# Gradient clipping by global norm: smaller last pieces, two engines for the squares, and a shorter scalar chain between load and store

## Chip, cores, metric

One NeuronCore of a Trainium2 chip. The metric is the device time of one execution in microseconds (us). Executions of one kernel agree within some 0.3 to 0.6%. A profile's span (50.5 us for the kernel before) is about 1.8 us shorter than the time of the same run. In the profile's lines PE is TensorE (PEld its weight load), DVE is VectorE, ACT ScalarE, POOL GpSimd and SP SyncE, whose queue issues the transfers; a q behind an engine's name is its sequencer, and L47 is line 47 of that run's kernel. A transfer has landed when its semaphore (the counter that those who need the data wait for) says so. The dots in the profile's fences mark lines left out.

## The reference

```python
grad: (512, 4096) float32      # 8.39 MB
norm  = np.sqrt(np.sum(grad ** 2))
scale = min(1.0, max_norm / (norm + 1e-8))     # max_norm = 1.0
return (grad * scale).astype(np.float32)
```

Every output needs the sum over every input. The whole tensor fits in SBUF, so it is read once and written once.

## The kernel before

```python
F = 2048                                     # nch = 8 chunks of [128, 2048], 1 MB each
gin = flat_in.rearrange("(n p f) -> n p f", p=P, f=F)
...
nc.vector.memset(ones, 1.0)
...
for i in range(nch):                         # 8 loads of 1 MB
    ch = data_pool.tile([P, F], fp32, name=f"ch{i}", tag="ch")
    chunks.append(ch)
    nc.sync.dma_start(out=ch, in_=gin[i])

for i in range(nch):                         # sums of squares, all on VectorE (line 47)
    nc.vector.tensor_tensor_reduce(out=sq, in0=chunks[i], in1=chunks[i], scale=1.0, scalar=0.0,
        op0=mult, op1=add, accum_out=acc[:, i : i + 1])

nc.vector.tensor_reduce(out=s, in_=acc, axis=X, op=add)           # over the 8 columns
nc.tensor.matmul(tot_psum, ones, s, start=True, stop=True)        # over the 128 partitions
nc.scalar.activation(out=nrm, in_=tot_psum, func=Sqrt)
nc.vector.tensor_scalar(out=nrm_eps, in0=nrm, scalar1=1.0e-8, scalar2=None, op0=add)
nc.vector.reciprocal(out=inv, in_=nrm_eps)
nc.vector.tensor_scalar(out=scl, in0=inv, scalar1=float(max_norm), scalar2=1.0, op0=mult, op1=min)

for i in range(nch):                         # scale (line 86) and store
    nc.vector.tensor_scalar(out=chunks[i], in0=chunks[i], scalar1=scl, scalar2=None, op0=mult)
    nc.sync.dma_start(out=gout[i], in_=chunks[i])
```

## Time and profile before

Median 52.33 us of 6 runs (52.23 to 52.41). The lines of the profile are in the prediction below; the table has only the lengths of the five stretches, from the first and last data packets of each block in the trace's DMA records.

| stretch of the kernel before | us |
|---|---|
| start of span to first byte of the load | 1.73 |
| load: first byte to last byte | 20.73 |
| hole: last byte of the load to issue of the first store | 5.86 |
| issue of the first store to its first byte | 0.85 |
| store: first byte to last byte | 20.18 |
| end: last byte to end of the span | 1.17 |

Read it as a sum: the stretches lie one behind another, and all but the load and the store are time in which no byte of the tensor moves. The prediction counts the hole from the moment at which the landing is seen (5.40 us); the table counts from the last byte, 0.46 us earlier.

### The profile page before, as it was taken

Reading aid. Unit: us, or ns where it says so; the run is one execution under the profiler, and the core shown is the slowest. Engines: PE = TensorE matmul, PEld = TensorE weight load, DVE = VectorE, ACT = ScalarE, POOL = GpSimd, SP = SyncE. Lnnn points to the kernel's source line nnn. Section 1 sums busy time; section 2 is a strip of 40 time slices with the busy share of each in tenths; the row PEclk is TensorE's granted clock in tenths of the full one; section 3 lists DMA queues with packets and bytes.
Section 4 is the critical chain, followed back from the end, with each engine's and each line's share of the span. In section 5 each row is a group of like instructions: output and inputs, shape, how many; then the busy total and the mean of one; then the engine's idle time right before and its main releaser. Section 6 shows DMA issues by size and latency. Waiting matters only on the chain.

```text
span 50.5 us, 112 instructions
## 1 busy us (share of the span) xinstructions
PE 0.6 (1%) x2; PEld 0.5 (1%) x2; DVE 28.9 (57%) x29; ACT 1.5 (3%) x2; POOL 0.2 (0%) x4
## 2 busy tenths in 40 slices
PE   0000000000000000000040000000000000000000
PEld 0000000000000000000030000000000000000000
DVE  1000597989898989898929999999900000000000
ACT  4500000000000000000010000000000000000000
POOL 1000000000000000000000000000000000000000
DMA  0679999999999999950000099999999999999980
GB/s 0 104 337 435 448 422 422 422 422 422 435 415 435 441 422 422 428 214 0 0 0 0 0 415 415 415 415 415 415 415 415 415 415 428 428 422 415 435 363 0
DMA packets 2304, 16.78 MB, mean 332 GB/s; under 512 B 256, under 2 KB 256, under 8 KB 256
## 3 DMA queue, kind: packets, MB, share of 16 engines
q1 hardware_dynamic: 2304, 16.78, 80.6%
HBM read 8.39 MB, written 8.39 MB: 332 GB/s over the span
## 4 chain that ended last, share of the span: by engine, by line
DMA 37%; DVE 23%; SPq 6%; DVEq 2%; issue 1%; PE 1%; ACT 0%
DMA ch<-in_grad_dram 37%; DVE ch L86 17%; SPq L44 6%; DVE sq L47 5%; DVEq L124 2%; PE tot L63 1%; ACT nrm L66 0%; DVE inv L74 0%; DVE s L59 0%; DVE nrm_eps L70 0%; DVE scl L76 0%; DVEq L47 0%; DVE acc L47 0%
## 5 line engine op out<-in xcount | busy, mean ns | idle before, releaser
L47 DVE CUSTOM_DVE_ANT_0 sq<-ch 128x2048 f32<-128x2048 f32 x8 | 18.3, 2293 | 6.0 <-DMA ch<-in_grad_dram 6.0
L86 DVE TENSOR_SCALAR ch<-ch,scl 128x2048 f32<-128x2048 f32 x8 | 9.7, 1281 | 0.0
L66 ACT ACT_TABLE_LOAD x1 | 1.3, 1283 | 0.7 <-PEq L110 0.7
L63 PE MATMUL tot<-s,ones 128*128 128x1 f32 x2 | 0.6, 361 | 25.6 <-DVE s L59 25.6
L66 ACT ACTIVATE nrm<-tot 128x1 f32<-128x1 f32 x1 | 0.2, 171 | 24.2 <-PE tot L63 24.2
L63 PEld LDWEIGHTS tot<-s,ones 128*128 128x128 f32 x2 | 0.5, 309 | 25.6 <-DVE s L59 25.6
L47 DVE DVE_READ_ACCUMULATOR2_ANT acc<- 128x1 f32 x8 | 0.7, 83 | 0.0
L70 DVE TENSOR_SCALAR nrm_eps<-nrm 128x1 f32<-128x1 f32 x1 | 0.2, 154 | 0.9 <-ACT nrm L66 0.9
L36 DVE MEMSET ones<- 128x128 f32 x1 | 0.2, 165 | 0.8 <-PEq L110 0.8
L74 DVE RECIPROCAL inv<-nrm_eps 128x1 f32<-128x1 f32 x1 | 0.2, 163 | 0.0
L59 DVE TENSOR_REDUCE s<-acc 128x1 f32<-128x8 f32 x1 | 0.2, 161 | 0.0
L76 DVE TENSOR_SCALAR scl<-inv 128x1 f32<-128x1 f32 x1 | 0.2, 153 | 0.0
L110 POOL MEMSET const-bfloat16-1.0<- 128x1 bf16 x1 | 0.1, 101 | 0.0
L110 POOL MEMSET const-uint8-127<- 128x1 uint8 x1 | 0.1, 101 | 0.0
L110 POOL MEMSET const-float32-0.0<- 128x1 f32 x1 | 0.1, 98 | 0.2 <-issue 0.2
L110 POOL MEMSET const-float32-1.0<- 128x1 f32 x1 | 0.1, 98 | 0.0
## 6 DMA issues: line engine op xcount, KB each, us to landing
ch<-in_grad_dram SPq DMA_DIRECT2D x8, 1024.0 KB, 11.8
out_dram<-ch SPq DMA_DIRECT2D x8, 1024.0 KB, 8.5
```

The source lines that it names most:

```text
L36: nc.vector.memset(ones, 1.0)
L44: nc.sync.dma_start(out=ch, in_=gin[i])
L47: nc.vector.tensor_tensor_reduce(out=sq, in0=chunks[i], in1=chunks[i], scale=1.0, scalar=0.0, op0=mybir.AluOpType.mult, op1=mybir.AluOpTyp ...
L59: nc.vector.tensor_reduce(out=s, in_=acc, axis=mybir.AxisListType.X, op=mybir.AluOpType.add)
L63: nc.tensor.matmul(tot_psum, ones, s, start=True, stop=True)
L66: nc.scalar.activation(out=nrm, in_=tot_psum, func=mybir.ActivationFunctionType.Sqrt)
L70: nc.vector.tensor_scalar(out=nrm_eps, in0=nrm, scalar1=1.0e-8, scalar2=None, op0=mybir.AluOpType.add)
L74: nc.vector.reciprocal(out=inv, in_=nrm_eps)
L76: nc.vector.tensor_scalar(out=scl, in0=inv, scalar1=float(max_norm), scalar2=1.0, op0=mybir.AluOpType.mult, op1=mybir.AluOpType.min,)
L86: nc.vector.tensor_scalar(out=chunks[i], in0=chunks[i], scalar1=scl, scalar2=None, op0=mybir.AluOpType.mult,)
L110: nc = _bacc.Bacc("TRN2", target_bir_lowering=False, num_devices=1)
L124: with _tile.TileContext(nc) as tc:
```

## The change

Its intent is to shorten the hole. The last chunk is cut in two regions of 1024 columns, and the squares of every chunk or region are shared between VectorE and ScalarE, so that little work is left when the last byte has landed. The scalar chain has two VectorE links instead of three. The first region stored is the last that was loaded, in two halves of 512 columns, so that the first store can be issued early. Memsets go to GpSimd, and a dummy square root loads ScalarE's table.

```diff
-    gin = flat_in.rearrange("(n p f) -> n p f", p=P, f=F)
+    widths = [F] * (nch - 1) + [1024, 1024]       # contiguous regions of HBM
...
-    nc.vector.memset(ones, 1.0)
+    nc.gpsimd.memset(ones, 1.0)
+    nc.gpsimd.memset(acc, 0.0)                    # acc has 12 columns
+    sq_v, sq_a = ... bf16                         # scratch output of the squares
+    nc.scalar.activation(out=dummy, in_=dummy, func=Sqrt)
...
-    for i in range(nch): tensor_tensor_reduce(chunks[i])           # VectorE
+    for i in range(6):                            # sq_accum: VectorE, sq_accum_act: ScalarE
+        (sq_accum_act if i % 2 else sq_accum)(chunks[i])
+    sq_accum(chunks[6][:, 0:1024]);  sq_accum_act(chunks[6][:, 1024:2048])
+    sq_accum(chunks[7][:, 0:512]);   sq_accum_act(chunks[7][:, 512:1024])
+    sq_accum(chunks[8][:, 0:576]);   sq_accum_act(chunks[8][:, 576:1024])
...
-    nrm = sqrt(tot); nrm_eps = nrm + 1e-8; inv = 1 / nrm_eps; scl = min(inv * max_norm, 1)
+    nrm = sqrt(tot / (mn * mn)); r = max(nrm, 1); scl = 1 / r
...
+    for c0, c1 in ((0, 512), (512, 1024)):
+        scale_store(chunks[8][:, c0:c1], view(flat_out, 8)[:, c0:c1])
+    for i in (7, 0, 1, 2, 3, 4, 5, 6):
+        scale_store(chunks[i], view(flat_out, i))
```

(Shortened to one line per step; each step is one instruction as in the code above.)

More of the change, by code (lines that the diff above doesn't have):

```diff
@@ L19 @@
     fp32 = mybir.dt.float32
+    bf16 = mybir.dt.bfloat16
     P = nc.NUM_PARTITIONS
+    mn = float(max_norm)
     flat_in = grad.flatten()
@@ L27, with view @@
     nch = total // (P * F)
-    gin = flat_in.rearrange("(n p f) -> n p f", p=P, f=F)
-    gout = flat_out.rearrange("(n p f) -> n p f", p=P, f=F)
-    data_pool = ctx.enter_context(tc.tile_pool(name="data", bufs=nch))
+    widths = [F] * (nch - 1) + [1024, 1024]
+    regions, at = [], 0
+    for w in widths:
+        regions.append((at, w))
+        at += P * w
+    assert at == total
+    def view(flat, r):
+        o, w = regions[r]
+        return flat[o : o + P * w].rearrange("(p f) -> p f", f=w)
@@ L32 @@
+    data_pool = ctx.enter_context(tc.tile_pool(name="data", bufs=1))
     small_pool = ctx.enter_context(tc.tile_pool(name="small", bufs=1))
     psum_pool = ctx.enter_context(tc.tile_pool(name="psum", bufs=1, space=bass.MemoryType.PSUM))
-    ones = small_pool.tile([P, P], fp32, name="ones")
-    nc.vector.memset(ones, 1.0)
-    acc = small_pool.tile([P, nch], fp32, name="acc")
-    sq = small_pool.tile([P, F], fp32, name="sq")
-    chunks = []
-    for i in range(nch):
-        ch = data_pool.tile([P, F], fp32, name=f"ch{i}", tag="ch")
-        chunks.append(ch)
-        nc.sync.dma_start(out=ch, in_=gin[i])
@@ L46 @@
-    for i in range(nch):
+    add = mybir.AluOpType.add
+    mult = mybir.AluOpType.mult
+    maxop = mybir.AluOpType.max
+    Sqrt = mybir.ActivationFunctionType.Sqrt
+    Square = mybir.ActivationFunctionType.Square
+    NR = len(widths)
+    chunks = [
+        data_pool.tile([P, w], fp32, name=f"ch{i}", tag=f"ch{i}")
+        for i, w in enumerate(widths)
+    ]
+    for i in range(NR):
+        nc.sync.dma_start(out=chunks[i], in_=view(flat_in, i))
+    ones = small_pool.tile([P, P], fp32, name="ones")
@@ L47, with sq_accum @@
+    nc.gpsimd.memset(ones, 1.0)
+    NACC = 12
+    acc = small_pool.tile([P, NACC], fp32, name="acc")
+    nc.gpsimd.memset(acc, 0.0)
+    sq_v = small_pool.tile([P, F], bf16, name="sq_v")
+    sq_a = small_pool.tile([P, F], bf16, name="sq_a")
+    dummy = small_pool.tile([P, 1], fp32, name="dummy")
+    nc.gpsimd.memset(dummy, 1.0)
+    nc.scalar.activation(out=dummy, in_=dummy, func=Sqrt)
+    ai = 0
+    def sq_accum(src):
+        nonlocal ai
+        n = src.shape[1]
         nc.vector.tensor_tensor_reduce(
-            out=sq,
@@ L49 @@
-            in0=chunks[i],
-            in1=chunks[i],
+            out=sq_v[:, 0:n],
+            in0=src,
+            in1=src,
             scale=1.0,
             scalar=0.0,
-            op0=mybir.AluOpType.mult,
-            op1=mybir.AluOpType.add,
-            accum_out=acc[:, i : i + 1],
-        )
-    s = small_pool.tile([P, 1], fp32, name="s")
-    nc.vector.tensor_reduce(
-        out=s, in_=acc, axis=mybir.AxisListType.X, op=mybir.AluOpType.add
-    )
+            op0=mult,
+            op1=add,
@@ new lines, in sq_accum, with sq_accum_act @@
+            accum_out=acc[:, ai : ai + 1],
+        )
+        ai += 1
+    def sq_accum_act(src):
+        nonlocal ai
+        n = src.shape[1]
+        nc.scalar.activation(
+            out=sq_a[:, 0:n],
+            in_=src,
+            func=Square,
+            accum_out=acc[:, ai : ai + 1],
+        )
+        ai += 1
+    for i in range(6):
+        (sq_accum_act if i % 2 else sq_accum)(chunks[i])
+    sq_accum(chunks[6][:, 0:1024])
+    sq_accum_act(chunks[6][:, 1024:2048])
+    sq_accum(chunks[7][:, 0:512])
@@ L62 @@
+    sq_accum_act(chunks[7][:, 512:1024])
+    sq_accum(chunks[8][:, 0:576])
+    sq_accum_act(chunks[8][:, 576:1024])
+    assert ai == NACC
+    s_col = small_pool.tile([P, 1], fp32, name="s_col")
+    nc.vector.tensor_reduce(out=s_col, in_=acc, op=add, axis=mybir.AxisListType.X)
     tot_psum = psum_pool.tile([P, 1], fp32, name="tot")
-    nc.tensor.matmul(tot_psum, ones, s, start=True, stop=True)
+    nc.tensor.matmul(tot_psum, ones, s_col, start=True, stop=True)
     nrm = small_pool.tile([P, 1], fp32, name="nrm")
-    nc.scalar.activation(
-        out=nrm, in_=tot_psum, func=mybir.ActivationFunctionType.Sqrt
-    )
@@ L69 @@
-    nrm_eps = small_pool.tile([P, 1], fp32, name="nrm_eps")
-    nc.vector.tensor_scalar(
-        out=nrm_eps, in0=nrm, scalar1=1.0e-8, scalar2=None, op0=mybir.AluOpType.add
-    )
-    inv = small_pool.tile([P, 1], fp32, name="inv")
-    nc.vector.reciprocal(out=inv, in_=nrm_eps)
-    scl = small_pool.tile([P, 1], fp32, name="scl")
-    nc.vector.tensor_scalar(
-        out=scl,
-        in0=inv,
-        scalar1=float(max_norm),
-        scalar2=1.0,
-        op0=mybir.AluOpType.mult,
-        op1=mybir.AluOpType.min,
-    )
@@ L85 @@
-    for i in range(nch):
-        nc.vector.tensor_scalar(
-            out=chunks[i],
-            in0=chunks[i],
-            scalar1=scl,
-            scalar2=None,
-            op0=mybir.AluOpType.mult,
-        )
-        nc.sync.dma_start(out=gout[i], in_=chunks[i])
+    nc.scalar.activation(out=nrm, in_=tot_psum, func=Sqrt, scale=1.0 / (mn * mn))
+    r = small_pool.tile([P, 1], fp32, name="r")
+    nc.vector.tensor_scalar(out=r, in0=nrm, scalar1=1.0, scalar2=None, op0=maxop)
+    scl = small_pool.tile([P, 1], fp32, name="scl")
@@ L97, with scale_store @@
+    nc.vector.reciprocal(out=scl, in_=r)
+    def scale_store(view_sb, view_hbm):
+        nc.vector.tensor_scalar(
+            out=view_sb, in0=view_sb, scalar1=scl, scalar2=None, op0=mult
+        )
+        nc.sync.dma_start(out=view_hbm, in_=view_sb)
+    for c0, c1 in ((0, 512), (512, 1024)):
+        scale_store(chunks[8][:, c0:c1], view(flat_out, 8)[:, c0:c1])
+    for i in (7, 0, 1, 2, 3, 4, 5, 6):
+        scale_store(chunks[i], view(flat_out, i))
 _INS = ['grad', 'max_norm']
```

## The prediction

> **What bounds the kernel now.** I read four views in this order: the page's forty slices, the stretches that I cut out of them, the groups of instructions, and the chain of work that ended last with the queue's own waits. First the slices (each is 50.5/40 = 1.26 us; the digit is the busy share in tenths):
>
> ```profile
> DVE  1000597989898989898929999999900000000000
> ACT  4500000000000000000010000000000000000000
> DMA  0679999999999999950000099999999999999980
> ```
>
> The transfers are busy at nine tenths or more in two blocks, the load and the store, with a hole of about five slices between. VectorE works under the load and in the hole; ScalarE has almost nothing to do. Cutting at the edges of the blocks gives (columns: stretch, length, busy time of PE, weight load, DVE, ACT, POOL, clock, DMA share, GB/s):
>
> ```profile
> 2.00:22.60 20.60, 0.00 (x0) 0.00 (x0) 15.82 (x13) 0.01 (x1) 0.00 (x0) 1.00 0.97 404
> 22.60:29.10 6.50, 0.58 (x2) 0.50 (x2) 5.31 (x10) 0.17 (x1) 0.00 (x0) 1.00 0.00 0
> 29.10:49.40 20.30, 0.00 (x0) 0.00 (x0) 7.56 (x7) 0.00 (x0) 0.00 (x0) 1.00 1.00 413
> ```
>
> So the span is two saturated transfers of 8.39 MB and 6.5 us with no byte moving. The sum can't be had without first having the whole tensor, so load and store can't overlap: time = start + load + hole + store + end, and a change can win only in the hole (or at the ends). What is in the hole is told by the chain in order of time (start, length, what):
>
> ```profile
> 4.29 18.63 DMA ch<-in_grad_dram
> ...
> 23.05 2.29 DVE sq L47
> 25.35 0.02 DVE acc L47
> ...
> 25.39 0.17 DVE s L59
> ...
> 25.61 0.60 PE tot L63 x2
> ...
> 26.23 0.18 ACT nrm L66
> ...
> 26.43 0.17 DVE nrm_eps L70
> 26.62 0.17 DVE inv L74
> 26.81 0.16 DVE scl L76
> ...
> 27.00 1.29 DVE ch L86
> ```
>
> The last load is seen to land at 4.29 + 18.63 = 22.92; the square-and-sum of that chunk then runs alone for 2.29 us, the scalar work takes from 25.39 to 26.98, the first scaling of a whole chunk 1.29, and the first store is issued at 28.32 by the timeline. Landing to first issue is 28.32 - 22.92 = 5.40 us. The rest of the 6.5 is receipt of the load and start-up of the store, which the change doesn't touch. The groups say what the two large pieces cost per instruction:
>
> ```profile
> L47 DVE CUSTOM_DVE_ANT_0 sq<-ch 128x2048 f32<-128x2048 f32 x8 | 18.3, 2293 | 6.0 <-DMA ch<-in_grad_dram 6.0
> L86 DVE TENSOR_SCALAR ch<-ch,scl 128x2048 f32<-128x2048 f32 x8 | 9.7, 1281 | 0.0
> L66 ACT ACT_TABLE_LOAD x1 | 1.3, 1283 | 0.7 <-PEq L110 0.7
> ```
>
> A chunk's squares take 2.29 us; a chunk lands about every 2.49 us (8.39 MB at the 422 GB/s that most slices show is 19.9 us for eight). VectorE therefore keeps up with the load, and only its last chunk shows. The table load is at the very start, under the first transfer, already now.
>
> **What the Trainium skill says.** (1) "VectorE: DVE Perf Modes", section "The perf-mode tier table": fp32 tensor_tensor in SBUF runs at one element per cycle (2293 ns for 2048), fp32 tensor_scalar at two (1227 ns). The trace agrees: 2293 for the square-and-sum, 1281 for the scaling, though a scaling starts every 1.195 us (7.17 us for six in the chain). So time falls with width: at 0.96 GHz 2293 ns is 2048 cycles + 153, and 1281 ns is 1024 cycles + 206. (2) "ScalarE: Activation LUTs", sections "What ACT_TABLE_LOAD costs" and "Table sets": an ACTIVATE with immediate operands takes 186 ns + 0.833 ns per element; a table load some 1283 ns, plus a drain; a set holds several functions, and cheap ones are in every set. The trace agrees on the load (1283) and roughly on the small ACTIVATE (171 at one element); it has no wide ACTIVATE. (3) "DMA: Bandwidth & Descriptors", section "Why small descriptors are slow": a packet has a fixed overhead of about 3 cycles beside its 32-byte beats. The trace before has only 8 KB data rows, so it doesn't test it; (1024 KB each, 2048 of the 2304 packets.)
>
> **The change part by part.**
> - Squares of chunks 0 to 5 alternating between VectorE and ScalarE, bf16 scratch output: VectorE goes from 18.3 us under the load to about half. Worth 0: it was keeping up. The bf16 output doesn't change the mode, since the inputs are fp32. By the skill a 2048-wide Square is 186 + 1706 = 1.89 us, every second chunk, so ScalarE keeps up too.
> - The last chunk is cut in two regions of 1024, and the last region split 576 columns to VectorE and 448 to ScalarE. VectorE: (576 + 153)/0.96 = 0.76 us where there were 2.29. ScalarE: 186 + 0.833 x 448 = 0.56, and something to bring out the accumulator; I take 0.25 (an estimate without a row behind it; VectorE's own accumulator read is 83 ns), so 0.81. Region 7 lands about 1.24 us earlier and its halves (0.69 and 0.86 us) are done by then. From landing: 0.13 to start, as before (22.92 to 23.05), then max(0.76 + 0.05, 0.81 + a semaphore) = 0.85. The reduce starts at landing + 0.98; before, 2.47. Saved 1.49.
> - Scalar chain: nrm_eps, inv, scl (26.43 to 27.00 = 0.57 us) become max and reciprocal, two links of 0.19: saved 0.19. The reduce over 12 instead of 8 columns is 4 cycles more. Sqrt with the constant folded in costs the same. Reduce start to scaling start: 27.00 - 25.39 - 0.19 = 1.42.
> - The first scaling is 512 columns, in the two-per-cycle mode: (256 + 206)/0.96 = 0.48 us where there were 1.28: saved 0.80, with the same 0.03 to the issue.
> - Sum: landing to first issue = 0.98 + 1.42 + 0.48 + 0.03 = 2.91, against 5.40: saved 2.49.
> - What it adds: rows of 4 KB in regions 7 and 8 and of 2 KB in the two half stores, one more load, two more stores. A row of 8 KB on one of 16 engines takes about 2.48/8 = 0.31 us; 256 beats at the page's 850 MHz are 0.30, so I put the overhead of a packet at 8 ns (an estimate from both). Load: 8 more packets per engine, 0.06 us. Stores: 4 more for region 7, 12 for region 8, 0.13 us. Three more completions, some 0.01 each. Added about 0.22.
> - Do the small stores feed the engines? An issue takes 0.35 us when nothing is queued (0.34 to 0.39 for the first ones), data flow begins 0.8 us after it (28.32 to 29.1). Call the first issue 0. 256 KB move in 0.62 us, so store one flows 0.8 to 1.42; store two is issued at 0.40 (the scaling's spacing, 1.195 - 0.80) and ready at 1.2; store three, 1024 columns, at 1.06, ready at 1.86 before 2.05; store four at 2.26, ready at 3.06 before 3.3. No gap, by 0.2 us each time.
> - The memsets on GpSimd and the warm-up Sqrt lie under the first transfer: 0.
>
> Total: 52.33 - 2.49 + 0.22 = 50.06, and I say 50.1.
>
> **Rivals.**
> - A second table load. If Square isn't in the set that the warm-up Sqrt loads, the final Sqrt reloads in the hole: 1.28 us and a drain, and the time is 51.4 to 52. For: the kernel has never used Square. Against: the skill counts cheap functions as in every set, and the warm-up is put there for this. Chance 5%.
> - ScalarE ends last instead of VectorE. Nothing in the trace shows an accumulator read there; each 0.1 beyond my 0.25 adds 0.1. If 0.5 us, 50.4.
> - The ninth load waits. The queue's own waits show that the ninth transfer (now the first store) waits for the first load:
>
> ```profile
> SPq L93 <- DMA ch<-in_grad_dram: 0.8, 1, 0.8
> ```
>
> The ninth is now a load: it would be issued at about 5.6 instead of 4.8, 15 us ahead of its turn in the line. Worth 0. Stores nine and ten would likewise wait for stores one and two, long landed.
> - Narrow rows or gaps eat it. If 2 KB rows moved at half speed the two half stores would cost 1.2 us more, and the time would be 51.2; a slip of 0.2 at the hand-over of the small stores becomes a gap. Against: large margins in the overhead estimate. Chance that it takes over 0.6: 6%.
> - Transfers hide it all: not possible, since none runs in the hole.
>
> **Range and chances.** The saving has three terms that rest on measured rows (1.49, 0.19, 0.80), good to about 0.2 together, and costs that can be 0 to 0.6. That gives 49.7 to 50.7. The line for 2% is 51.28, 1.2 us above the prediction; only the table reload or a badly slow row gets there. Faster 0.95, within 2% 0.04, slower 0.01.
>
> **What would show it.** In the changed profile: one table load, at the start; square-and-sum of 576 columns about 0.76 us and the 448-column Square near 0.56, the reduce starting 1.0 us after the last landing; two VectorE links between Sqrt and the first scaling; a first scaling of 0.48; landing to first issue 2.9; idle transfers about 4.0 us instead of 6.5; load and store blocks as long as before within 0.1 and 0.2. The prediction is wrong if a table load or a long accumulator read stands in the hole, if the store block has a gap in its first 3 us, or if the last landing moves later by more than 0.2.

## The result, and the profile after

The changed kernel takes 50.46 us (median of 8 runs, 50.39 to 50.53) against 52.36 (16 runs of the kernel before on the same chips): 1.90 us less. The ratio is 0.9642 (95% interval 0.9631 to 0.9654). Here and below a ratio is the mean time of one kernel's runs over the mean of the other's runs of the same rounds, so not quite the ratio of the medians quoted. Executions over 1.5% slower than the fastest of the same kernel are left out of the means. It is outside the 2% that count as the same.

The stretches of the changed kernel (start, length, busy time per engine, clock, DMA share, GB/s):

```profile
2.00:22.70 20.70, 0.00 (x0) 0.00 (x0) 8.83 (x10) 8.09 (x12) 0.00 (x0) 1.00 0.97 402
22.70:26.80 4.10, 0.56 (x2) 0.50 (x2) 2.53 (x8) 0.84 (x3) 0.00 (x0) 1.00 0.00 0
26.80:47.20 20.40, 0.00 (x0) 0.00 (x0) 8.63 (x8) 0.00 (x0) 0.00 (x0) 1.00 1.00 411
47.20:48.60 1.40, 0.00 (x0) 0.00 (x0) 0.00 (x0) 0.00 (x0) 0.00 (x0) 1.00 0.00 0
```

The stretch with no byte moving fell from 6.5 to 4.1 us, 2.4 less. The kernel gained only 1.9, so something was given back, in three places. From the DMA records of the two traces:

| stretch, us | before | after | difference |
|---|---|---|---|
| start | 1.73 | 1.73 | 0 |
| load | 20.73 | 20.84 | +0.11 |
| hole | 5.86 | 3.46 | -2.40 |
| issue to first byte | 0.85 | 0.85 | 0 |
| store | 20.18 | 20.36 | +0.18 |
| end | 1.17 | 1.41 | +0.24 |
| span | 50.51 | 48.65 | -1.87 |

The chain of the changed kernel through the hole (start, length, what):

```profile
5.59 17.43 DMA ch<-in_grad_dram
...
23.15 0.76 DVE sq_v L77
...
24.02 0.17 DVE s_col L111
...
24.33 0.57 PE tot L113 x2
...
24.93 0.18 ACT nrm L116
...
25.13 0.17 DVE r L118
25.32 0.17 DVE scl L120
...
25.52 0.49 DVE ch L123
```

Landing is seen at 5.59 + 17.43 = 23.02. The reduce starts 1.00 us later (2.47 before), the scaling starts 1.50 us after the reduce (1.61 before), and the first store is issued at 26.03 (by the timeline): 3.01 us from landing to issue, 5.40 before. Look at the step from the reduce's end to the matmul: 24.02 + 0.17 = 24.19 to 24.33 is 0.14 us; before it was 0.05 (25.56 to 25.61). That is the first odd point.

The groups of instructions, by form (line, engine, operation, out<-in, shapes, count | busy us, mean ns of one | idle us before it):

```profile
L92 ACT ACTIVATE sq_a<-ch 128x448 bf16<-128x448 f32 x1 | 0.6, 576 | 0.5 <-DMA ch<-in_grad_dram 0.5
L92 ACT ACTIVATION_READ_ACCUMULATOR sq_a<-ch 128x1 f32 x6 | 1.1, 186 | 0.0
L70 ACT ACT_TABLE_LOAD x1 | 1.3, 1283 | 0.7 <-PEq L148 0.7
```

There is one table load, at the start: Square and Sqrt share a set here. ScalarE's last piece ends at 23.77 by the timeline (23.58 + 0.19), VectorE's at about 23.91, so VectorE's still ends last. The second odd point is at the end. These are the waits of SyncE's queue in the end (total, times, longest), first in the kernel before, then in the changed one:

```profile
SPq L124 <- DMA out_dram<-ch: 12.0, 5, 2.5
```

```profile
SPq L162 <- DMA out_dram<-ch: 11.4, 1, 11.4
```

Before, the queue waits five times, each for a transfer that lands about 2.5 us after the one before it. Changed, it waits once, for 11.4 us, and that is the last transfer; the other semaphores come behind it in the list.

### The profile page after: what moved, and what is told of

It is laid out like the page before. It is cut to its first block, busy times and chain, and to the rows that moved or that the text cites.

```text
span 48.6 us, 134 instructions
## 1 busy us (share of the span) xinstructions
PE 0.6 (1%) x2; PEld 0.5 (1%) x2; DVE 20.0 (41%) x25; ACT 10.2 (21%) x15; POOL 0.5 (1%) x7
## 4 chain that ended last, share of the span: by engine, by line
DMA 46%; DVE 22%; PE 1%; issue 1%; DVEq 1%; ACT 0%
DMA ch<-in_grad_dram 46%; DVE ch L123 20%; DVE sq_v L77 2%; PE tot L113 1%; DVEq L162 1%; ACT nrm L116 0%; DVE s_col L111 0%; DVE scl L120 0%; DVE r L118 0%; DVEq L111 0%; DVEq L77 0%; DVE acc L77 0%
## 5 line engine op out<-in xcount | busy, mean ns | idle before, releaser
L77 DVE CUSTOM_DVE_ANT_0 sq_v<-ch 128x2048 bf16<-128x2048 f32 (+3 forms) x6 | 9.6, 1592 | 14.3 <-DMA ch<-in_grad_dram 14.3
L92 ACT ACTIVATE sq_a<-ch 128x2048 bf16<-128x2048 f32 (+3 forms) x6 | 8.0, 1332 | 13.0 <-DMA ch<-in_grad_dram 12.9
L123 DVE TENSOR_SCALAR ch<-ch,scl 128x2048 f32<-128x2048 f32 (+2 forms) x10 | 9.9, 1068 | 0.0
L92 ACT ACTIVATION_READ_ACCUMULATOR sq_a<-ch 128x1 f32 x6 | 1.1, 186 | 0.0
L113 PE MATMUL tot<-s_col,ones 128*128 128x1 f32 x2 | 0.6, 348 | 24.3 <-DVE s_col L111 24.3
L113 PEld LDWEIGHTS tot<-s_col,ones 128*128 128x128 f32 x2 | 0.5, 310 | 24.3 <-issue 24.3
```

The costliest lines, as they stand in the source:

```text
L77: nc.vector.tensor_tensor_reduce(out=sq_v[:, 0:n], in0=src, in1=src, scale=1.0, scalar=0.0, op0=mult, op1=add, accum_out=acc[:, ai : ai + 1],)
L92: nc.scalar.activation(out=sq_a[:, 0:n], in_=src, func=Square, accum_out=acc[:, ai : ai + 1],)
L113: nc.tensor.matmul(tot_psum, ones, s_col, start=True, stop=True)
L123: nc.vector.tensor_scalar(out=view_sb, in0=view_sb, scalar1=scl, scalar2=None, op0=mult)
```

## The experiments

Theories: (1) the gain comes only from the tail of the load and the head of the store, where each part's worth is its width or its number of links; (2) what was given back is packets (rows) in the two blocks, the order of waits at the end, and a second wait ahead of the matmul. Rivals are in the expectations. Every kernel gave the correct result. Time of the kernel before in the three sets of runs: 52.38, 52.35 and 52.35. In the tables "hole" is always last byte of the load to first issue.

### The end: which semaphore the last store counts on

Both edits add tiny loads (16 x 64 elements) that nobody reads, behind the real loads. The transfers take eight semaphores in turn, so the edits shift the last store to another one.

```diff
     for i in range(nch): ... nc.sync.dma_start(...)      # kernel before: 8 + 3 + 8 = 19 transfers
+    for j in range(3): nc.sync.dma_start(out=junk_j, in_=grad[0:16, 0:64])
     for i in range(NR): nc.sync.dma_start(...)           # changed kernel: 9 + 5 + 10 = 24 transfers
+    for j in range(5): nc.sync.dma_start(out=junk_j, in_=grad[0:16, 0:64])
```

> The kernel before with three tiny loads (4 KB each) issued behind the real loads, so 19 transfers as in the changed kernel, and the last store counts on the same semaphore as there. Theory A (the 0.21 us after the last byte come from the order in which the end waits for the semaphores): the last byte to the end of the span grows from 1.17 to about 1.36 us (three more waits of 0.063 behind the one that is released last), time 52.36 + 0.2 = 52.55. Theory B (they come from the number of transfers): the same here, so this run alone doesn't tell A from B; it does tell both from C. Theory C (they come from the narrow rows or from something on other engines): no growth, 52.36.

> The changed kernel with five tiny loads, so 24 transfers, and the last store counts on the semaphore that is waited for last. Theory A (order of waits): last byte to the end of the span falls from 1.38 to about 1.17 us, time 50.46 - 0.2 = 50.25. Theory B (number of transfers): it grows further, to 1.5 or more, time 50.6. Theory C: no change, 50.46.

| | end, us | time, us | ratio to before |
|---|---|---|---|
| before | 1.17 | 52.38 | |
| before with 19 transfers | 1.34 | 52.65 | 1.0052 (1.0037 to 1.0066) |
| changed | 1.41 | 50.46 | 0.9642 |
| changed with 24 transfers | 1.18 | 50.38 | 0.9615 (0.9597 to 0.9634) |

The queue's waits at the end, of the kernel before with 19 transfers, then of the changed one with 24:

```profile
SPq L128 <- DMA out_dram<-ch: 12.2, 1, 12.2
```

```profile
SPq L166 <- DMA out_dram<-ch: 11.2, 5, 2.5
```

The pattern of waits swapped, and the length of the end with it. More transfers gave the shorter end, so theory B (their number) falls, and the kernel before got the longer end without narrow rows or another engine's work, so theory C falls too. In the traces, four semaphore instructions about 0.063 us apart follow the released one in the changed kernel, three in the kernel before with 19 transfers, and none in the other two. Both times came out 0.1 above what was expected of theory A (52.65 for 52.55, 50.38 for 50.25). With 24 transfers the time moved less than the end did (0.08 instead of 0.23), since the load block of that profile was 0.1 us longer, 20.93. Load blocks of otherwise like kernels here range from 20.74 to 20.93, so from a time alone an effect below 0.1 us can't be settled; whether the tiny loads themselves lengthen the load block is not separated from this scatter. The end's length is settled.

### The rows

```diff
-    gin = flat_in.rearrange("(n p f) -> n p f", p=P, f=F)
+    gin = flat_in.rearrange("(n a p f) -> n p a f", a=2, p=P, f=F // 2)    # and gout alike
```

> The kernel before with every transfer cut into rows of 4 KB on the HBM side and nothing else: the same 16 transfers, the same compute. Theory A (a packet has a fixed cost: the changed kernel's 4 KB load packets take 160.5 ns against 309 for 8 KB, 12 ns more per pair, its stores 161.5 against 313, 10 more): 64 pairs per engine and direction, load block +0.77, store block +0.64, time 52.36 + 1.4 = 53.75. Theory B (the longer blocks of the changed kernel, +0.11 and +0.18, are the cost of one and two more transfers, about 0.1 each): no change, 52.36.

53.67 us, ratio 1.0261 (1.0240 to 1.0282): 1.29 us slower. Load block +0.73 (20.73 to 21.45), store block +0.76 (20.18 to 20.94), hole and end unchanged. The data packets double from 2048 to 4096 (with 256 small ones, 2304 before and now):

```profile
DMA packets 4352, 16.78 MB, mean 322 GB/s; under 512 B 256, under 2 KB 256, under 8 KB 4352
```

Number and order of the transfers are those of the kernel before, so the cost lies in the packets: 0.73 and 0.76 us over 64 added packets per engine and direction are 11 to 12 ns each. That profile is of the slowest of the five runs (53.91); by the median, 1.29 us over 128 packets, it is 10 ns. The edit also changes where in HBM a partition's two rows lie, which no run separates. The changed kernel's regions are contiguous; it adds 16 packets in the store (0.16 to 0.19 by this), which is what its store block grew by, 0.18. In the load it adds 8 (0.08 to 0.10); the 0.11 there fits, but is no larger than the scatter of the load blocks.

### The wait ahead of the matmul

```diff
-    nc.gpsimd.memset(ones, 1.0)
+    nc.vector.memset(ones, 1.0)
```

> The changed kernel with the memset of the ones matrix back on VectorE. In the changed kernel TensorE has a semaphore instruction of 51 ns ahead of the weight load, and 0.14 us pass between the reduce and the matmul where there were 0.04. Theory A (the matmul now waits for two engines, VectorE and GpSimd, and the second wait is an instruction of its own in the hole): the gap falls to 0.04, time 50.46 - 0.09 = 50.37. Theory B (the gap is something else, such as an idle TensorE): no change, 50.46.

The chain of this kernel:

```profile
24.07 0.18 DVE s_col L111
...
24.29 0.60 PE tot L113 x2
```

From the reduce's end to the matmul is now 0.04 us, and TensorE's extra semaphore instruction is gone: theory A. In the hole it is 0.07 (3.40 against 3.46). The time is 50.46 (ratio 0.9637, 0.9620 to 0.9655), no different: an effect of 0.07 us lies below what the runs resolve, so the mechanism is shown in the trace and its worth in time is not.

### Each part of the hole

The early chunks, all on VectorE again:

```diff
-        (sq_accum_act if i % 2 else sq_accum)(chunks[i])        # i in 0..5
+        sq_accum(chunks[i])
```

> The changed kernel with the squares of chunks 0 to 5 all on VectorE, as in the kernel before. Theory A (the split of these chunks between two engines is hidden under the load): last byte of the load to first store issue stays 3.46 us, time 50.46. Theory B (VectorE carries a backlog from the early chunks into the last ones, so the split is part of the gain): the reduce comes 0.1 to 0.5 us later and the time is 50.6 to 50.9.

The last two regions squared together:

```diff
-    sq_accum(chunks[7][:, 0:512]); sq_accum_act(chunks[7][:, 512:1024])
-    sq_accum(chunks[8][:, 0:576]); sq_accum_act(chunks[8][:, 576:1024])
+    sq_accum(last[:, 0:1152]);     sq_accum_act(last[:, 1152:2048])   # one tile, two loads
```

> The changed kernel, same transfers, but the last two regions lie in one tile and are squared together once both have landed, 1152 columns on VectorE and 896 on ScalarE: the finer grain of the tail is undone, the split between engines kept. Theory A (time falls with width at 0.96 GHz): the square of 1152 takes 1.36 us instead of 0.76, last byte to issue 3.46 + 0.60 = 4.06, time 51.06. Theory B (the landing or a fixed cost sets the reduce, not the width): under 0.2 more.

The last two regions on one engine:

```diff
-    sq_accum(chunks[7][:, 0:512]); sq_accum_act(chunks[7][:, 512:1024])
-    sq_accum(chunks[8][:, 0:576]); sq_accum_act(chunks[8][:, 576:1024])
+    sq_accum(chunks[7]);           sq_accum(chunks[8])
```

> The changed kernel with the last two regions (1024 columns each) squared by VectorE alone: the split between engines is undone, the grain kept. Theory A: 1.23 us instead of 0.76 for the last, less 0.06 for the wait on ScalarE ahead of the reduce that goes: last byte to issue 3.46 + 0.41 = 3.87, time 50.87. Theory B (ScalarE with its 0.19 us accumulator read is what the reduce waits for in the changed kernel, so the split is worth little): 0.2 or less, time under 50.66.

The first store whole (with one tiny load, so that the end stays the same):

```diff
-    for c0, c1 in ((0, 512), (512, 1024)):
+    for c0, c1 in ((0, 1024),):
```

> The changed kernel with the last region scaled and stored in one piece of 1024 columns instead of two of 512 (one tiny load added, so there are still 19 transfers and the end is the same). Theory A: the first scaling takes 0.75 us instead of 0.48, last byte to issue +0.27; the store block is shorter by 16 packets of 86 ns less 8 of 162 = 0.08 and one completion; time 50.46 + 0.18 = 50.64. Theory B (the hand-over of the small stores leaves a gap, or narrow rows cost more than their packets show): the store block shrinks by 0.3 or more and the time is 50.4 or less.

The three links of before:

```diff
-    r = max(nrm, 1); scl = 1 / r
+    nrm_eps = nrm + 1e-8; inv = 1 / nrm_eps; scl = min(inv * mn, 1)    # and no scale in the square root
```

> The changed kernel with the three VectorE links of before (add of the epsilon, reciprocal, multiply and min) between square root and first scaling instead of two. Theory A (a dependent link costs 0.19 us whatever it computes): last byte to first issue 3.46 + 0.19 = 3.65, time 50.65. Theory B (the links overlap in part): under 0.1 more.

| changed kernel with | hole, us | store block, us | time, us | ratio to before |
|---|---|---|---|---|
| nothing undone | 3.46 | 20.36 | 50.46 | 0.9642 |
| early chunks on VectorE | 3.52 | 20.38 | 50.45 | 0.9636 (0.9623 to 0.9650) |
| last regions squared together | 4.07 | 20.36 | 51.01 | 0.9744 (0.9731 to 0.9757) |
| last regions on VectorE alone | 3.95 | 20.35 | 50.89 | 0.9721 (0.9707 to 0.9735) |
| first store whole | 3.77 | 20.26 | 50.68 | 0.9679 (0.9666 to 0.9692) |
| three links | 3.66 | 20.35 | 50.63 | 0.9666 (0.9653 to 0.9679) |

The chains give the step that moved. First the early chunks on VectorE, where the last square is unmoved in length (the 0.06 in the hole is a later sight of the landing: the square starts 0.64 us after the last byte instead of 0.58):

```profile
23.18 0.76 DVE sq_v L77
```

Then the last regions squared together:

```profile
23.17 1.36 DVE sq_v L79
```

Then VectorE alone:

```profile
23.08 1.23 DVE sq_v L77
```

Then the first scaling with the store whole:

```profile
25.57 0.75 DVE ch L127
```

And the three links:

```profile
25.18 0.17 DVE nrm_eps L118
25.37 0.17 DVE inv L120
25.57 0.17 DVE scl L122
```

So: sharing the early chunks is worth nothing (0.01 us, inside the noise). The finer grain of the tail is worth 0.55 us of time, 0.60 of hole, with the two engines kept. The second engine in the tail is worth 0.43 of time, 0.49 of hole, with the grain kept; one of five runs of that kernel (51.61) was slow and is left out of the table's 50.89. For the hole 0.41 had been expected: 0.47 for the longer square, less 0.06 for a wait on ScalarE ahead of the reduce. That wait did not go: in this kernel's trace the reduce still waits for two engines, since ScalarE has earlier pieces, and the semaphore instruction (21 ns) still stands ahead of it. The halves of the first store win 0.31 in the hole, of which some 0.26 is the shorter scaling, give back 0.10 in the store block, and leave 0.22 of time. One link is 0.19 in the hole, 0.17 of time. These values are for undoing one part at a time and don't have to add up to the whole, since grain and second engine shorten the same stretch. Nor does this undo the whole change: the first scaling's step from 2048 to 1024 columns (1.29 to 0.75 us in the chains) was undone by no run, and neither were the bf16 scratch, the dummy square root and the order of the stores, so their worth is not shown. The square of 2048 columns takes 2292 ns with the bf16 scratch and 2293 without, and the kernel before had its one table load at the start without a dummy.

### Putting the findings to use

Three kernels have the ones on VectorE, a last load region of 512 columns (304 to VectorE, 208 to ScalarE), every early chunk shared by both engines, and a number of transfers that puts the last store on the semaphore waited for last. They differ in their widest rows and in the tiny loads that fill up the number:

```diff
-    widths = [F] * 7 + [1024, 1024]
+    widths = [F] * 7 + [1024, 512, 512]                   # narrow: rows to 8 KB, 24 transfers, 4 tiny
+    widths = [4096, 4096, F, F, F, 1024, 512, 512]        # rows to 16 KB, 16 transfers, none tiny
+    widths = [8192, F, F, F, 1024, 512, 512]              # rows to 32 KB, 16 transfers, 2 tiny
+    for i in reversed(range(len(widths))): scale_store(...)   # the widest last
```

> What the runs so far suggest, without wide rows: ones memset on VectorE, a last load region of 512 columns (304 on VectorE, 208 on ScalarE), every chunk split between both engines, four tiny loads so that there are 24 transfers and the last store counts on the semaphore waited for last. From measured parts: hole 3.46 - 0.10 (TensorE's wait) - 0.20 (ScalarE's 208 columns end it) = 3.16; load block +0.1 for the 2 KB rows; end 1.17 instead of 1.41; time about 50.05. Rival: the narrow rows and the extra transfers give back what the hole wins, 50.4.

> The same as narrow_24 in hole and end, but two loads and two stores are 4096 columns wide (rows of 16 KB), and there are 16 transfers, none of them tiny. Theory A (each packet has a fixed cost of about 12 ns, whatever its length): 16 packets fewer per engine and direction, 0.19 us less in the load block and in the store block, time about 49.65. Theory B (a row over 8 KB is cut into packets of 8 KB, or has the same time per byte): 50.05.

> The same, with one load and one store of 8192 columns (rows of 32 KB) in place of the two of 4096, and two tiny loads for 16 transfers. Theory A: 8 packets fewer again per engine and direction, 0.1 us less in each block, time about 49.45. Theory B (no gain above 16 KB, or the wide store has to wait for its 4.8 us of scaling and leaves a gap): 49.65 or more.

| | load | hole | store | end | time | ratio to before |
|---|---|---|---|---|---|---|
| rows to 8 KB | 20.95 | 3.15 | 20.37 | 1.18 | 50.06 | 0.9559 (0.9546 to 0.9572) |
| rows to 16 KB | 21.21 | 3.12 | 20.18 | 1.18 | 50.09 | 0.9565 (0.9552 to 0.9578) |
| rows to 32 KB | 20.71 | 3.12 | 20.10 | 1.18 | 49.61 | 0.9475 (0.9454 to 0.9497) |

The first hit its mark. Rows of 16 KB shortened the store block by the 0.19 expected and made the load block longer by 0.26: a miss, 50.09 for an expected 49.65. Rows are not cut into 8 KB packets: the records show 16 KB packets of 613 ns (median), so theory B is wrong too. The loss is in the start of the load, first the kernel with 8 KB rows, then with 16 KB (columns as above):

```profile
3.00:4.00 1.00, 0.00 (x0) 0.00 (x0) 0.00 (x0) 0.00 (x0) 0.00 (x0) 1.00 1.02 426
```

```profile
3.00:4.00 1.00, 0.00 (x0) 0.00 (x0) 0.00 (x0) 0.00 (x0) 0.00 (x0) 1.00 0.69 295
```

In that microsecond the engines move 295 GB/s instead of 426. Counting packets in flight by their share, 0.49 MB had arrived at 4.00 us, against 0.61 with 8 KB rows and 0.62 with 32 KB; at 12.00 us it was 3.93 against 4.02, so the loss is in the start and most of it stays. Why a load that starts with two transfers of 16 KB rows ramps up more slowly, while one that starts with 32 KB rows is not behind at 4 us, stays open; there is one profile of each, though the times of all five runs agree with it. The 32 KB kernel is the fastest, 2.74 us under the kernel before and about 0.85 under the changed one. Its 49.61 lies between the two theories' 49.45 and 49.65 and decides for neither: its four runs spread from 49.49 to 49.77, and the profile is of the fastest. A gap for the wide scaling is not seen, since its store block is the shortest, 20.10.

## Why the prediction was right

Predicted 50.1 (49.7 to 50.7), measured 50.46: inside the range, on the side of too little cost. Its steps:

- **What bounds the kernel, and that only the hole can win**: right for this change. All of the gain, 2.40 us, is in the hole. The end and the rows can be won from too, as the experiments show, by some 0.2 us each.
- **Sharing the early chunks is worth 0**: right, shown by the experiment with those chunks on VectorE.
- **The tail's squares**: reduce at landing + 0.98 predicted, 1.00 measured, in part by luck. The 0.76 us for 576 columns was 0.758. The prediction let ScalarE end last, with 0.81 of work and a semaphore, 0.85. ScalarE's work was 0.67: 576 ns for the square and 186 for the accumulator read, which overlap by about 0.09. VectorE ended last, and from the start of its square to the reduce it took 0.87 (23.15 to 24.02) where the prediction had 0.81, since a semaphore instruction stands ahead of the reduce. The two misses nearly cancel.
- **Two links instead of three, 0.19**: right; restoring the third gave 0.19 in the hole.
- **Reduce to scaling, 1.42**: 1.50 measured. The term left out is the matmul's second wait, since the memset had been moved to GpSimd. I had put the memsets down as 0, "under the first transfer"; the work is, the wait isn't.
- **First scaling of 512 columns, 0.48**: 0.49.
- **Sum, landing to issue**: 2.91 predicted, 3.01 measured.
- **Rows and completions, 0.22**: 0.29 measured (0.11 and 0.18). I put a packet at 8 ns; the experiment with 4 KB rows gives 10 to 12. The 0.11 is within the scatter of the load blocks.
- **The end, 0**: wrong by 0.24, the largest miss. I had read that transfers share eight semaphores and asked only whether issues would wait for them, not in what order the end waits for them.
- **Rivals**: no second table load; ScalarE did not end last; the ninth load waits 0.8 us without effect; no gap between the small stores (the second and third stretches of the profile after have a DMA share of 0.00 and 1.00).

From 50.06 by the unrounded sum to 50.46 are 0.40 us: 0.10 in landing to issue, 0.07 in the blocks, 0.24 at the end.

## What to carry to other kernels

When load and store are both saturated and one needs all of the other, cut only what lies between the last landing and the first store: the width of the last piece per engine, each dependent link, the width of the first piece; work under the load can be left as it is. When you move a small set-up instruction to another engine or change the number of transfers, look at which waits that adds at the join and at the end, since they are paid one behind another after the last landing. Make the bulk rows wide and only the pieces at the hand-over narrow, and measure the start of the load when you do: of the two widths tried here one gained and one did not.

## What the Trainium skill lacked or had wrong

- "ScalarE: Activation LUTs", section "What ACT_TABLE_LOAD costs" (the durations of an ACTIVATE): it has no cost for the accumulator output. Here each accumulating ACTIVATE has an ACTIVATION_READ_ACCUMULATOR of 186 ns behind it, and takes 17 ns more than the page's 186 + 0.833 N with immediates (576 against 559 at 448 columns; 1909 against 1892 at 2048).
- "DMA: Bandwidth & Descriptors", section "Why small descriptors are slow": about 3 cycles per packet are 3.5 ns at the page's 850 MHz (an estimate from the page); for the descriptor's 32 bytes, the other cost it names, it gives no time. The experiment with 4 KB rows shows 10 to 12 ns for each added packet, near the 10.5 ns per packet that the page's section "Bandwidth" has for a 4 KB transfer issued from GpSimd. No section says what row width costs: here rows of 4 KB instead of 8 KB cost 1.29 us of 52.4.
- "DMA: Bandwidth & Descriptors", section "Latency and other measured facts": first byte after some 600 ns on this path, without saying from where it counts. Here the first data packet starts 0.85 us after the start of the first store's issue and 1.00 us after the first load's (0.73 to 1.73); from the end of the issue, 0.35 and 0.38 us later, it is 0.50 and 0.62 us.
- "Perfetto Trace Analysis", section "Identifying Dependency Chains", says that an instruction that waits for several engines may have semaphore instructions ahead of it, but not what they cost (here about 0.1 us from reduce to matmul). No page that I found has the semaphore instructions that follow the last landing at the end (four of 0.063 us; the end 1.41 against 1.17 and 1.18 us).
- Agreement, for completeness: one element per cycle plus about 150 cycles in "VectorE: DVE Perf Modes" gives 0.757 us at 576 columns (an estimate from the page); the trace shows 0.758.
